# The second layer's input projection in seven half-depth products for eight, its operands, v, gates and decays waiting in DRAM

## The chip, the cores and the metric

The kernel runs on one core of a Trainium2 chip. A core has the engines TensorE (PE in the profile, with its weight loads as PEld), VectorE (DVE), ScalarE (ACT), GpSimd (POOL) and SyncE (SP), which here only issues DMAs. The metric is the time of one execution on the device in microseconds (us), less being better, given as the median of several runs. The profile is taken from one further execution.

## The reference: what is computed

An encoder of two layers works on 2048 tokens of width 1024. The first (even) layer mixes by a gated linear recurrence and short convolutions. The second (odd) one is a bidirectional gated linear attention with 4 heads; key width 128 and value width 256 per head. The part that matters:

```python
def odd_layer(x, norm_pre, norm_post, w_in, w_gate_lr, b_gate, head_norm_g, w_out):
    h = rmsnorm(x, norm_pre)
    proj = h @ w_in
    q, k, v, r, lr = jnp.split(
        proj, [GLA_KEY, 2 * GLA_KEY, 2 * GLA_KEY + GLA_VAL, 2 * GLA_KEY + 2 * GLA_VAL], axis=-1)
    ...
    z = jnp.einsum('bsdr,drk->dbsk', lr, w_gate_lr...) + b_gate[...]
    log_alpha = jax.nn.log_sigmoid(z) / GLA_NORMALIZER
    ...
    o_f = gla_chunked(qh, kh, vh, g_f)
    o_b = jnp.flip(gla_chunked(jnp.flip(qh, 2), ..., jnp.flip(g_b, 2)), 2)
    o = rmsnorm(o_f + o_b, head_norm_g)
    y = (o * jax.nn.silu(r.astype(jnp.float32))) @ w_out
    return (x + rmsnorm(y, norm_post)).astype(x.dtype)
```

`w_in` of this layer has 3104 columns: q and k (512 each), v and r (1024 each) and a rank part lr of 32, from which the decays `log_alpha` are made. x is 1024 wide on 2048 tokens.

## The kernel before

Activations lie transposed, with features on the 128 partitions and tokens along the free axis, in four chunks of 512 tokens. An fp32 operand of a projection is split into two f16 halves, hi and lo; a product is then three matmuls: weight hi by hi, weight hi by lo, weight lo by hi.

The stages, in order: the even layer's input projection, already made in seven half-depth products for eight (`mm3`, lines 794 to 796), with its operands waiting in DRAM; recurrences and convolutions beside it; the even output (`wo_mm`, lines 1123 to 1125), 1536 matmuls over chunks 0 to 3, each of eight groups (m) of 48 matmuls; beside it `post_even`, which norms each chunk, adds the residual and makes the operands H2 (hi, lo) of the second layer; the second layer's projections, `proj_atom` (lines 607, 608, 610) for q, k, r and the rank part, and `v_atom` (lines 1335 to 1337) for v; per head, `phase1` makes the decays from the rank part (a scan along the tokens, lines 1480 and 1483) and multiplies q and k by their exponentials, and `gla` makes scores (line 1557), transposes, states (1589) and outputs (1633, 1649, 1651); `gpost` and `gpost_out` norm a head's output, multiply by the gate and save it to DRAM; finally the output product (`wq_mm`, lines 1807 to 1809) with `post_odd` beside it.

The order of all instructions is made when the program is built. Each step of the work is a generator that says which engine it needs next ("P" TensorE, "A" ScalarE, "V" VectorE, "G" GpSimd, "D" a DMA) and for how long by a table of costs, and which events it waits for. The planner `Order` always takes the step that can start earliest, and among equals the one of better priority. Buffers come from pools: 22 large slots of 8 KB per partition with a cap for each role (H2 8, XR 2, V 3, E 4 and so on), eight PSUM banks, raw weight slots and pieces for split weights. The engines run their lists strictly in that order. All DMAs are on one queue, SP's, and are issued at line 279; line 250 is the helper of all ScalarE operations, 254 and 258 those of VectorE's.

The projections of the second layer serve as filler: the planner lays products of later heads between the attention matmuls of the present one. Weights are loaded and split (`WO`, `hl`, `WX` in the profile: high half by ScalarE, low half by VectorE) shortly ahead of their use. The gates r of head 3 are the last products in this order; `gate3` takes them. After the last head, `wq_split` splits the eight output weights.

Of the kernel before, what the change touches and what calls it, by code (L numbers as in the profile page):

```python
# [17 lines left out]
T = 2048  # L18
# [3 lines left out]
NSLOT = 22  # L22
# [135 lines left out]
def trunk_kernel(ctx: ExitStack, tc: tile.TileContext, xT, w_in, gate_w, w_out, odd_w, lr_w, lr_gw, odd_wo, params, outT):  # L158
# [18 lines left out]
        WO=8, YC=6, YB=2, XR=2, H2=8, LM=1, V=3, WX=2, QS=2, E=4, SB=1, O=2, G3=2, YL=1,  # L177
# [153 lines left out]
    def lam_consts():  # L331
# [25 lines left out]
        nc.vector.tensor_scalar(out=gsc[:, 16:24], in0=par[:, C_OPRE:C_OPRE + 8], scalar1=-2.0 ** -23, scalar2=None,  # L357
# [37 lines left out]
    pc_left = {i: 2 if i < 3 else 4 for i in range(5)}  # L395
# [16 lines left out]
    def pc_drop(i):  # L412
        pc_left[i] -= 1
        if pc_left[i] == 0:
            (wput if i < 3 else put)(PCT[i])
# [178 lines left out]

    def proj_atom(key, c, w, hh, cls="bg", ev2=None):
        b = yield from bank(cls)
        n = 0
        for hf in range(2):
            if hf and ev2 is not None:
                yield ("w", ev2)  # L600
            three = key[0] != "lr"
            yield ("P", (12 if three else 8) * 0.216)
            for kk in range(4):
                k = hf * 4 + kk
                hi, lo = hh[c][hf].t[:, kk, 0], hh[c][hf].t[:, kk, 1]
                wh, wl = w.s.t[:, 0, k], w.s.t[:, 1, k]
                nc.tensor.matmul(b.t, lhsT=wh, rhs=hi, start=(n == 0), stop=False)  # L607
                nc.tensor.matmul(b.t, lhsT=wh, rhs=lo, start=False, stop=(n == 7 and not three))  # L608
                if three:
                    nc.tensor.matmul(b.t, lhsT=wl, rhs=hi, start=False, stop=(n == 7))  # L610
                n += 1
        P[key, c] = b
        done(evP[key, c])
# [487 lines left out]
    def yc_loader():  # L1101
        yield ("w", evAlloc)
        for c in range(NCH):
            if c >= 2:
                yield ("w", evH2[c - 2])
            for q in range(4):
                s = yield from get("YC", [128, 4, 2, CH], F16)
                YC[c, q] = s
                for j in range(4):
                    ki = q * 4 + j  # L1110
                    yield ("w", evY[ki])
                    yield from dma(s.t[:, j], y_d[ki][:, :, c * CH:(c + 1) * CH], 256 * 1024)
                    done(evYC[c, ki])
# [53 lines left out]
    H2 = [[None, None] for _ in range(NCH)]  # L1167
    evH2 = [Ev() for _ in range(NCH)]
    XR = {}
    evXR = {(c, h): Ev() for c in range(NCH) for h in range(2)}  # L1170

    def xr_loader():
        yield ("w", evAlloc)
        yield ("w", ev_proj)
        for c in range(NCH):
            for hf in range(2):
# [17 lines left out]
    def post_even():  # L1194
        yield ("w", ev_proj)
        for c in range(NCH):
            yb = []
            for _ in range(2):
                s = yield from get("YB", [128, 4, CH])
                yb.append(s)  # L1200
# [19 lines left out]
            put(yb[1])  # L1220
            yield from rsq(r, b, 1.0 / (1024 * 4096), 1)
            put(yb[0])
            for hf in range(2):
# [3 lines left out]
                h = yield from get("H2", [128, 4, 2, CH], F16)  # L1227
                H2[c][hf] = h
                yield from act(h.t[:, :, 0], x, AF.Copy)
                yield from tt(h.t[:, :, 1], x, h.t[:, :, 0], ALU.subtract)  # L1230
                put(XR[c, hf])
# [12 lines left out]
    odd_order = [("lr", 0)]  # L1244
    for hd in range(4):
        if hd == 0:
            odd_order += [("q", hd), ("k", hd), ("va", hd), ("vb", hd)]
        if hd + 1 < 4:
            odd_order += [("q", hd + 1), ("k", hd + 1)]
        if hd < 2:  # L1250
            odd_order += [("va", hd + 1), ("vb", hd + 1), ("r", 2 * hd), ("r", 2 * hd + 1)]
        if hd == 2:
            odd_order += [("va", hd + 1), ("vb", hd + 1)]
    odd_order += [("r", i) for i in (4, 5, 6, 7)]
    for key in odd_order:
# [12 lines left out]
    items_odd = [(key, osrc(key)) for key in odd_order]  # L1268
    W["wz", 0] = Wt()
    items_odd.insert(3, (("wz", 0), lr_gw))  # L1270
    WV = {}
    evXput = [Ev() for _ in range(4)]
    evGLA = [Ev() for _ in range(4)]
    evWV = [Ev() for _ in range(4)]

    def w_split_odd():
        yield ("w", ev_proj)
        for key, _ in items_odd:
            w = W[key]
            if key[0] == "wz":  # L1280
                yield ("w", ev_wodone)
                s = yield from get("LM", [128, 2 * T], F16)
                mask = s.t[:, T:T + T // 2].bitcast(U8)
                LM[0] = (s.t[:, 0:T], mask)
                wz = s.t[:, T + T // 2:2 * T].rearrange("p (d n) -> p d n", d=2)
                WZ[0] = wz
                yield ("G", 2.0)
                nc.gpsimd.memset(mask, 1)
                nc.gpsimd.memset(mask.rearrange("p (n t) -> p n t", t=128)[:, :, 0:1], 0)
# [5 lines left out]
                done(w.ev)  # L1295
                continue
            if key[0] in ("va", "vb"):
                hd = key[1]
                if key[0] == "va":
                    yield ("w", ev_wodone)  # L1300
                    WV[hd] = yield from get("WX", [128, 8, 2, 256], F16)
                yield ("w", w.evr)
                o = 0 if key[0] == "va" else 128
                t = WV[hd].t
                yield from act(t[:, :, 0, o:o + 128], w.raw.t, AF.Copy, scale=1024.0)
                yield from stt(t[:, :, 1, o:o + 128], w.raw.t, 1024.0, t[:, :, 0, o:o + 128], ALU.mult, ALU.subtract)
                wput(w.raw)
                if o:
                    done(evWV[hd])
            else:  # L1310
                yield ("w", w.evr)
                w.s = yield from wget("hl", [128, 2, 8, 128], F16)
                yield from act(w.s.t[:, 0], w.raw.t, AF.Copy, scale=1024.0)
                if key[0] == "lr":

                    lo = w.s.t[:, 1, :, 96:128]
                    yield from stt(lo, w.raw.t[:, :, 96:128], 1024.0, w.s.t[:, 0, :, 96:128], ALU.mult, ALU.subtract)
                    yield from act(w.s.t[:, 0, :, 96:128], lo, AF.Copy)
                else:
                    yield from stt(w.s.t[:, 1], w.raw.t, 1024.0, w.s.t[:, 0], ALU.mult, ALU.subtract)  # L1320
                wput(w.raw)
                done(w.ev)

    def v_atom(hd, tp):

        b = yield from bank("bg", (128, 2, 256))
        for i in range(2):
            tk = tp * 2 + i
            c, o = tk // 4, (tk % 4) * 128
            yield ("P", 24 * 0.1095)  # L1330
            for k in range(8):
                h = H2[c][k // 4].t
                hi, lo = h[:, k % 4, 0, o:o + 128], h[:, k % 4, 1, o:o + 128]
                wh, wl = WV[hd].t[:, k, 0], WV[hd].t[:, k, 1]
                nc.tensor.matmul(b.t[:, i], lhsT=hi, rhs=wh, start=(k == 0), stop=False)  # L1335
                nc.tensor.matmul(b.t[:, i], lhsT=hi, rhs=wl, start=False, stop=False)  # L1336
                nc.tensor.matmul(b.t[:, i], lhsT=lo, rhs=wh, start=False, stop=(k == 7))  # L1337
        VP[hd, tp] = b
        done(evV[hd, tp])

    VP = {}
    evV = {(hd, tp): Ev() for hd in range(4) for tp in range(8)}
    ev_oproj = Ev()

    def bg_odd():
        yield ("w", ev_proj)

        def mt(key, cs):
            yield ("w", W[key].ev)
            for c in cs:  # L1350
                yield ("w", evH2[c])
                yield from proj_atom(key, c, W[key], H2)
            if cs[-1] == NCH - 1:
                wput(W[key].s)

        def vt(hd, tps):
            yield ("w", evWV[hd])
            for tp in tps:
                yield ("w", evH2[tp // 2])
                yield from v_atom(hd, tp)  # L1360

        for key in odd_order[:3]:
            yield from mt(key, [0, 1, 2])
        S.pools["ps"]["caps"].update(bg=4, fg=4)
        S.logs = True
        yield from vt(0, range(6))
        for key in odd_order[:3]:
            yield from mt(key, [3])
        yield from vt(0, range(6, 8))
        put(WV[0])  # L1370

        def rt(hd):
            ka, kb = ("r", 2 * hd), ("r", 2 * hd + 1)
            yield ("w", W[ka].ev)
            yield ("w", W[kb].ev)
            for c in CORD:
# [612 lines left out]
```

## Time and profile before

| | |
|---|---|
| median of 3 runs | 2254.71 us (2252.21 to 2256.13) |
| profiled execution | 2253.91 us |
| its span | 2252.2 us |
| mean granted TensorE clock | 0.994 |
| TensorE, VectorE, ScalarE busy | 97%, 61%, 54% |
| moved by DMA | 279.75 MB, mean 124 GB/s |
| even output begins, ends | about 1026, 1371 us |
| last outputs of the last head | about 2022 us |
| output product begins | 2070 us |

How to read it: "busy" is the sum of the durations of an engine's instructions. TensorE's matmuls are pipelined, so that the duration of one (0.38 us) is longer than the pitch from start to start (0.216 us); the pitch is what a matmul costs in a full stream. A row of a group names line, engine, operation, tile written and tiles read, shape, count, busy time, mean ns of one, and then the idle time just ahead with what ended it. A row of a DMA names the tiles, the count, the KB of each and the median us from issue to landing.

### The profile page before, as it was taken

To read this page: it belongs to the slowest core of one execution; us is meant where nothing else is said; L and a number is where in the kernel's file an instruction comes from. 1 tells how busy PE (TensorE), PEld (TensorE's weight loads), DVE (VectorE), ACT (ScalarE), POOL (GpSimd) and SP (SyncE) were. 2 spreads that over 40 slices of the span, in tenths; PEclk is the share of its full clock that TensorE was granted. 3 is DMA by queue.
4 is the path that set the end of the run, shared out by engine and by line. 5 is a ranking of instruction groups with operands and counts; after the bars stand their busy time and mean duration, and the time that the engine had idled before them with its cause. 6 is when DMAs were issued, how large, how long until landed. Compare 5 with 4: busy or idle time off the path is not lost.

```text
span 2252.2 us, 27779 instructions
## 1 busy us (share of the span) xinstructions
PE 2194.3 (97%) x11658; PEld 1185.3 (53%) x11658; DVE 1376.6 (61%) x1501; ACT 1206.9 (54%) x1566; POOL 2.8 (0%) x8
## 2 busy tenths in 40 slices
PE   5889999999999999999999999999999999999997
PEld 4334444444444444444444444768559558774446
DVE  7988788886776767674234344453733734656535
ACT  5567777866667666664122222546536636556322
POOL 0000000000000000000000000000000000000000
PEclk9999999999999999999999999999999999999999
DMA  7354453554535445369232221100020020005433
GB/s 263 141 222 173 166 203 124 192 187 150 218 136 200 178 165 219 131 238 315 73 131 75 78 73 66 47 10 11 24 71 1 17 68 10 15 15 183 156 109 113
DMA packets 87886, 279.75 MB, mean 124 GB/s; under 512 B 6737, under 2 KB 43729, under 8 KB 67537
## 3 DMA queue, kind: packets, MB, share of 16 engines
q1 hardware_dynamic: 87760, 277.98, 34.2%
q8 instruction: 91, 1.49, 0.3%
q14 instruction: 35, 0.28, 0.0%
HBM read 221.33 MB, written 56.62 MB: 123 GB/s over the span
## 4 chain that ended last, share of the span: by engine, by line
PE 85%; DVE 9%; ACT 3%; DMA 2%; issue 1%; SPq 0%; DVEq 0%; ACTq 0%
PE ps L796 11%; PE ps L794 11%; PE ps L795 11%; PE ps L1123 5%; PE ps L1124 5%; PE ps L1125 5%; PE ps L607 4%; PE ps L608 4%; PE ps L610 4%; PE ps L1808 2%; PE ps L1807 2%; PE ps L1809 2%; PE ps L1589 2%; DVE E L258 2%; PE ps L1335 2%; PE ps L1336 2%
## 5 line engine op out<-in xcount | busy, mean ns | idle before, releaser
L794 PE MATMUL ps<-H,PC 128*128 128x512 f16 (+1 forms) x744 | 280.5, 377 | 3.7 <-DMA H<-hd 2.9
L796 PE MATMUL ps<-H,PC 128*128 128x512 f16 (+1 forms) x744 | 280.4, 377 | 1.5 <-DVE PC L254 1.4
L795 PE MATMUL ps<-H,PC 128*128 128x512 f16 (+1 forms) x744 | 280.4, 377 | 0.0
L794 PE MATMUL ps<-H,hl 128*128 128x512 f16 (+1 forms) x648 | 244.4, 377 | 10.6 <-ACT H L250 7.3
L795 PE MATMUL ps<-H,hl 128*128 128x512 f16 (+1 forms) x648 | 244.3, 377 | 6.5 <-DVE H L258 6.5
L796 PE MATMUL ps<-H,hl 128*128 128x512 f16 (+1 forms) x648 | 244.6, 377 | 4.5 <-DVE hl L254 4.4
L607 PE MATMUL ps<-H,hl 128*128 128x512 f16 x544 | 206.8, 380 | 0.6 <-ACT QS L250 0.6
L608 PE MATMUL ps<-H,hl 128*128 128x512 f16 x544 | 206.7, 380 | 0.0
L610 PE MATMUL ps<-H,hl 128*128 128x512 f16 x512 | 194.4, 380 | 0.0
L1123 PE MATMUL ps<-YC,WO 128*128 128x512 f16 x512 | 194.1, 379 | 0.0
L1124 PE MATMUL ps<-YC,WO 128*128 128x512 f16 x512 | 194.0, 379 | 0.0
L1125 PE MATMUL ps<-YC,WO 128*128 128x512 f16 x512 | 194.0, 379 | 0.0
L1335 PE MATMUL ps<-WX,H 128*128 128x256 f16 x512 | 139.6, 273 | 0.0
L1336 PE MATMUL ps<-WX,H 128*128 128x256 f16 x512 | 139.6, 273 | 0.0
L1337 PE MATMUL ps<-WX,H 128*128 128x256 f16 x512 | 139.6, 273 | 0.0
L150 ACT ACT_TABLE_LOAD x95 | 121.9, 1283 | 1.6
L794 PEld LDWEIGHTS <-PC 128*128 128x128 f16 x744 | 72.8, 98 | 91.5 <-DMA H<-hd 4.7
L796 PEld LDWEIGHTS <-PC 128*128 128x128 f16 x744 | 72.8, 98 | 88.8 <-DVE PC L254 2.9
L795 PEld LDWEIGHTS <-PC 128*128 128x128 f16 x744 | 72.8, 98 | 85.9 <-issue 0.3
L796 PEld LDWEIGHTS <-hl 128*128 128x128 f16 x648 | 64.5, 100 | 85.8 <-issue 9.2
L1807 PE MATMUL ps<-YC,WO 128*128 128x512 f16 (+1 forms) x320 | 107.7, 337 | 0.0
L1808 PE MATMUL ps<-YC,WO 128*128 128x512 f16 (+1 forms) x320 | 107.7, 336 | 0.0
(227 smaller groups left out, 4052.5 us busy)
## 6 DMA issues: line engine op xcount, KB each, us to landing
H<-hd SPq DMA_DIRECT2D x112, 1024.0 KB, 5.9
raw<-w_in SPq DMA_DIRECT2D x48, 512.0 KB, 4.3
yd<-YH SPq DMA_DIRECT2D x16, 1024.0 KB, 4.9
YC<-yd SPq DMA_DIRECT2D x64, 256.0 KB, 4.8
hd<-H SPq DMA_DIRECT2D x14, 1024.0 KB, 4.9
raw<-odd_w SPq DMA_DIRECT2D x24, 512.0 KB, 3.7
raw<-w_out SPq DMA_DIRECT2D x16, 512.0 KB, 5.3
XR<-xT SPq DMA_DIRECT2D x8, 1024.0 KB, 8.1
```

The costliest lines, as they stand in the source:

```text
L607: nc.tensor.matmul(b.t, lhsT=wh, rhs=hi, start=(n == 0), stop=False)
L608: nc.tensor.matmul(b.t, lhsT=wh, rhs=lo, start=False, stop=(n == 7 and not three))
L610: nc.tensor.matmul(b.t, lhsT=wl, rhs=hi, start=False, stop=(n == 7))
L794: nc.tensor.matmul(b.t[:, sl], lhsT=wh, rhs=hi, start=s, stop=False, skip_group_check=True)
L795: nc.tensor.matmul(b.t[:, sl], lhsT=wh, rhs=lo, start=False, stop=False, skip_group_check=True)
L796: nc.tensor.matmul(b.t[:, sl], lhsT=wl, rhs=hi, start=False, stop=e, skip_group_check=True)
L1123: nc.tensor.matmul(b.t, lhsT=wh, rhs=hi, start=start, stop=False)
L1124: nc.tensor.matmul(b.t, lhsT=wh, rhs=lo, start=False, stop=False)
L1125: nc.tensor.matmul(b.t, lhsT=wl, rhs=hi, start=False, stop=stop)
L1335: nc.tensor.matmul(b.t[:, i], lhsT=hi, rhs=wh, start=(k == 0), stop=False)
L1336: nc.tensor.matmul(b.t[:, i], lhsT=hi, rhs=wl, start=False, stop=False)
L1807: nc.tensor.matmul(out, lhsT=wh, rhs=hi, start=start, stop=False)
```

## The change

The second layer's projections of q, k, r and v are made in seven products of half depth for eight, as the even layer's are. For a pair of output tiles and a pair of token chunks the eight products of four K-tiles become seven, on sums and differences of operands and of weights. It has these parts.

- **Operands.** `op2_make` and `op2_rest` make seven operands (hi, lo; 1 MB each) for chunks 0 and 1, and seven for 2 and 3, and save all 14 to DRAM. The first use of each half takes them where they were made; the later eight blocks reload them (`op2_loader`, 56 loads of 1 MB). XR's cap goes from 2 to 4, since sums need two chunks at once.
- **Weights.** `w_prep` makes, beside the even output, the sums of all 12 pairs of weight tiles (4 sums and 7 splits each) and saves the pieces (98 saves; those of v as two saves of 256-byte runs per piece and pair). `wu_loader` reloads them in order, and begins when all are prepared.
- **Products.** `seven` issues the seven products; its `copies` (ScalarE) and `sums` (VectorE) empty the banks, of which a unit takes four.
- **Order of the blocks.** `OBLK` says by hand which units of which half of the tokens follow each other. The gates are no longer the last products to be laid between attention matmuls: `r_out` applies SiLU at once and saves them (8 x 1 MB), and `g_loader` reloads them per chunk into YL.
- **Decays** are all made ahead (`decays`, both directions at once, all four heads), saved (8 x 1 MB) and reloaded in `phase1`. **v** of heads 1 to 3 is saved and reloaded too.
- Slots go from 22 to 23. The loads of the output weights wait for `evRaw`, the end of the weight preparation; `yc_loader` issues its loads as threads of their own.

The diff, cut:

```diff
-NSLOT = 22
+NSLOT = 23
...
-        WO=8, YC=6, YB=2, XR=2, H2=8, LM=1, V=3, WX=2, QS=2, E=4, SB=1, O=2, G3=2, YL=1,
+        WO=8, YC=6, YB=2, XR=4, H2=3, LM=1, WV=4, V=2, VD=2, XS=1, QS=2, E=4, SB=1, O=2, DQ=2, YL=2,
...
+    def op2_make(x, j, src):
+        s = yield from get("H2", [128, 4, 2, CH], F16)
+        yield from act(s.t[:, :, 0], src.t, AF.Copy)
+        yield from tt(s.t[:, :, 1], src.t, s.t[:, :, 0], ALU.subtract)
+        OP2[x, j] = s
+        done(evOp2[x, j])
+        S.spawn(op2_save(x, j), 3)
...
+    OBLK = [(0, [("qk", 0), ("v", 0)]), (1, [("v", 0), ("qk", 0), ("v", 1)]), (0, [("v", 1), ("r", 0)]),
+            (1, [("r", 0), ("qk", 1)]), (0, [("qk", 1), ("r", 1)]), (1, [("r", 1), ("qk", 2)]),
+            (0, [("qk", 2), ("r", 2)]), (1, [("r", 2), ("qk", 3)]), (0, [("qk", 3), ("r", 3)]), (1, [("r", 3)])]
...
+                def op(j, src, evo=evo, u=u, i=i, last=i == len(prs) - 1):
+                    p = yield from pget()
+                    yield from wsplit(p, src)
+                    S.spawn(w_save(u, j, i, p, last), 3)
+                    done(evo[j])
...
+                yield ("w", ra.evr)
+                yield ("w", rb.evr)
+                a11, a12 = ra.raw.t[:, 0:4], ra.raw.t[:, 4:8]
+                a21, a22 = rb.raw.t[:, 0:4], rb.raw.t[:, 4:8]
+                S.spawn(op(0, a11), 3)
+                S.spawn(op(2, a12), 3)
+                yield from tt(s, a21, a22, ALU.add)
+                S.spawn(op(1, s), 3)
+                S.spawn(op(5, a22), 3)
+                yield from tt(a21, a11, a21, ALU.subtract)
...
+    def wu_loader():
+        yield ("w", evPrep)
...
+            for n, b, s, a, i, op in (("C11", "B", "s1", 0, 0, ALU.add), ("C12", "E", "s2", 0, 1, ALU.add),
+                                      ("U3", "A", "s5", 1, 1, ALU.add), ("U3", "A", "s4", 1, 0, ALU.subtract)):
...
+        prod = (("A", True, "P1", None), ("E", True, "P5", None), ("B", True, "C11", None), ("A", False, "U2", "s1"),
+                ("E", False, "C12", "s5"), ("D", True, "P4", None), ("A", False, "U3", "s2"))
...
+    def r_out(h, x, s):
+        yield from act(s.t, s.t, AF.Silu)
+        yield from dma(r_d[h][x], s.t.rearrange("p a i t -> p a (i t)"), 2 ** 20)
...
+    def phase1(hd, d):
+        yield ("w", evGd[3, 0])
+        yield ("w", evGd[3, 1])
...
+        yield from dma(t2.t, g_d[hd, d], 2 ** 20)
+        yield from act(t1.t, t2.t, AF.Exp, scale=-1.0 / 16)
+        yield from act(t2.t, t2.t, AF.Exp, scale=1.0 / 16)
...
     def wq_loader():
+        yield ("w", evRaw)
```

Two places show what moves. On TensorE, at the end of the attention: in the kernel before, the last outputs of head 3 (lines 1649 and 1651) are followed by 216 projection matmuls (lines 607, 608, 610), and then comes the output product (1807).

```order
L1649 MATMUL ps_14377<-WX_13832,V_13621 128x128
L1651 MATMUL ps_14377<-E_13430,SB_13835 128x128
L607 LDWEIGHTS hl_12822
L607 MATMUL ps_14373<-H_817_9509,hl_12822 128x512
L608 LDWEIGHTS hl_12822
L608 MATMUL ps_14373<-H_817_9509,hl_12822 128x512
```

The same place now; 1889 and 1891 are the outputs, 2034 to 2036 the output product, WO its split weights and YC the gated head outputs loaded from DRAM.

```order
L1889 MATMUL ps_15053<-XS_14490,V_14309 128x128
L1891 MATMUL ps_15053<-E_14304,SB_14493 128x128
L2034 LDWEIGHTS WO_1403_15074
L2034 MATMUL ps_14995<-YC_1402_15073,WO_1403_15074 128x512
L2035 LDWEIGHTS WO_1403_15074
L2035 MATMUL ps_14995<-YC_1402_15073,WO_1403_15074 128x512
```

No projection matmul stands between outputs and output product any more. On VectorE at the same place, the kernel before: the last outputs are added (QS, first two rows), then gating (O), splits of the output weights (WO<-raw) and one of a gate weight (hl<-raw) alternate.

```order
L258 TENSOR_TENSOR QS_13833<-ps_14377,QS_13833 128x128
L258 TENSOR_TENSOR QS_13834<-ps_14377,QS_13834 128x128
L254 SCALAR_TENSOR_TENSOR O_12846<-O_12846,gsc,hv_13226 128x512
L258 TENSOR_TENSOR O_12846<-ps_14160,O_12846 128x512
L254 SCALAR_TENSOR_TENSOR WO_1295_14407<-raw_13230,WO_1295_14407 128x1024
L254 SCALAR_TENSOR_TENSOR YL_14026<-O_12846,YL_14026 128x512
L254 SCALAR_TENSOR_TENSOR hl_14426<-raw_12852,hl_14426 128x1024
L254 SCALAR_TENSOR_TENSOR WO_1295_14407<-raw_14413,WO_1295_14407 128x1024
```

And now, with the norm of head 3 (hv, ps) and its gating (QS, YL) between the splits:

```order
L258 TENSOR_TENSOR QS_14491<-ps_15053,QS_14491 128x128
L258 TENSOR_TENSOR QS_14492<-ps_15053,QS_14492 128x128
L258 TENSOR_TENSOR ps_14960<-ps_14960,hv_14952 128x512
L254 SCALAR_TENSOR_TENSOR hv_14952<-ps_14960,hv_14952 128x512
L254 SCALAR_TENSOR_TENSOR QS_14491<-QS_14491,gsc,hv_14952 128x512
L258 TENSOR_TENSOR QS_14491<-YL_14953,QS_14491 128x512
L254 SCALAR_TENSOR_TENSOR WO_1403_15074<-raw_14653,WO_1403_15074 128x1024
L258 TENSOR_TENSOR hv_14952<-ps_15080,hv_14952 128x512
L254 SCALAR_TENSOR_TENSOR YL_14953<-QS_14491,YL_14953 128x512
L254 SCALAR_TENSOR_TENSOR QS_14492<-QS_14492,gsc,hv_14952 128x512
L258 TENSOR_TENSOR hv_15087<-hv_14952,hv_15087 128x512
L258 TENSOR_TENSOR QS_14492<-YL_14953,QS_14492 128x512
```

From the addition of the last outputs to the eighth split VectorE's list now has 37 instructions of 512 columns and 8 splits of 1024; the first lies behind the first chunk's norm and gating.

More of the change, by code (lines that the diff above doesn't have):

```diff
@@ L393, in pieces @@
         done(ev_pc)
-    pc_left = {i: 2 if i < 3 else 4 for i in range(5)}
+    pc_left = {i: 2 if i in (0, 1, 2, 5, 6, 7, 8, 9) else 4 for i in range(10)}
     pc_closing = set()
@@ L593, in trunk_kernel @@
     evP = {}
[L595 to L613, printed above, removed]
     first = [("xa", 0), ("gc", 0), ("xb", 0), ("zb", 0)]
@@ L1324, in v_atom @@
[L1324 to L1339, printed above, removed]
@@ new lines, in trunk_kernel, with op2_loader @@
+    WVS = {}
+    BL2 = {}
+    evBl2 = {(b, j): Ev() for b in range(len(OBLK)) for j in range(7)}
+    def op2_loader():
+        for b, (x, _) in enumerate(OBLK):
+            for j in range(7):
+                if b < 2:
+                    yield ("w", evOp2[x, j])
+                    BL2[b, j] = OP2[x, j]
+                else:
+                    if b == 2 and j == 0:
+                        S.pools["slot"]["caps"].update(H2=7)
+                    yield ("w", evH2d[x][j])
+                    BL2[b, j] = yield from get("H2", [128, 4, 2, CH], F16)
+                    S.spawn(fetch(BL2[b, j].t, h2_d[x][j], 2 ** 20, evBl2[b, j]), 2)
+                    continue
+                done(evBl2[b, j])
@@ new lines, in fetch, with lr_mm @@
+    def fetch(out, in_, nbytes, ev):
+        yield from dma(out, in_, nbytes)
+        done(ev)
+    def lr_mm(c):
+        x = c // 2
+        b = yield from bank("bg")
+        terms = [(0, 0), (0, 1), (1, 4)] if c % 2 else [(0, 0), (1, 2)]
+        yield ("w", evLRP)
+        for i, (hf, j) in enumerate(terms):
+            yield ("w", evBl2[x, j])
+            yield ("P", 8 * 0.2157)
+            op, w = BL2[x, j].t, LRP[hf].t
+            for k in range(4):
+                for a in range(2):
+                    nc.tensor.matmul(b.t, lhsT=w[:, 0, k], rhs=op[:, k, a], start=(i == 0 and k == 0 and a == 0),
+                                     stop=(i == len(terms) - 1 and k == 3 and a == 1))
+        P[("lr", 0), c] = b
+        done(evP[("lr", 0), c])
@@ new lines, in v_save, with unit_v, alloc, after @@
+    def v_save(h, x):
+        yield from dma(v_d[h][x], V[h][x].t, 2 ** 20)
+        put(V[h][x])
+        done(evVs[h][x])
+    def unit_v(p, blk, wfin, ofin):
+        x = OBLK[blk][0]
+        hs = (2 * p, 2 * p + 1)
+        def alloc():
+            for h in hs:
+                if V[h][x] is None:
+                    V[h][x] = yield from get("V" if h == 0 else "VD", [128, 8, 256])
+        def after():
+            for h in hs:
+                if h == 0:
+                    count(("v", 0), 4, lambda: done(evVd[0]))
+                else:
+                    count(("v", h, x), 2, lambda: S.spawn(v_save(h, x), 3))
+        for s in range(2):
+            def dst(a, i, s=s):
+                return V[hs[a]][x].t[:, 4 * i + 2 * s:4 * i + 2 * s + 2]
+            yield from seven(("v", p), blk, s, alloc, dst, (U12, U12), after, wfin, ofin and s == 1)
+        if wfin:
+            for s in WVS["v", p]:
+                put(s)
+            if p:
+                done(evWVd)
```

605 lines of the change are left out of this document (366 added, 239 removed).

## The prediction

> **What bounds the kernel now.** The page comes first. TensorE is busy for 97% of the span, and the chain of waits lies on it for 85%.
>
> ```profile
> span 2252.2 us, 27779 instructions
> PE 2194.3 (97%) x11658; PEld 1185.3 (53%) x11658; DVE 1376.6 (61%) x1501; ACT 1206.9 (54%) x1566; POOL 2.8 (0%) x8
> PE 85%; DVE 9%; ACT 3%; DMA 2%; issue 1%; SPq 0%; DVEq 0%; ACTq 0%
> ```
>
> The profiled execution took 2253.91 us, 1.7 more than its span and 0.8 less than the median of the runs, 2254.71. My sums are made against 2253.91. About 0.2%, 4.5 us, is what a measurement here tells from no change.
>
> An average over the span says nothing of one stage, so I cut it where the PE lines change: even output (from 1026), start of the second layer (1371), attention heads (1490), products left over after the last head (2023), output product (2070). The columns are the window, its length, then busy time and instructions of PE, weight load, VectorE (DVE), ScalarE (ACT) and GpSimd; then the granted clock, the DMA engines' share and GB/s.
>
> ```profile
> 1026.00:1371.00 345.00, 345.00 (x1598) 156.81 (x1597) 126.01 (x125) 92.33 (x114) 1.97 (x2) 1.00 0.32 107
> 1371.00:1490.00 119.00, 118.39 (x741) 72.65 (x740) 68.30 (x49) 55.19 (x67) 0.00 (x0) 1.00 0.17 57
> 1490.00:2023.00 533.00, 530.37 (x3555) 386.90 (x3554) 267.96 (x380) 283.52 (x477) 0.00 (x0) 1.00 0.08 24
> 2023.00:2070.00 47.00, 47.00 (x219) 21.49 (x218) 27.38 (x35) 27.99 (x40) 0.00 (x0) 1.00 0.52 161
> ```
>
> From 1026 to 2070 TensorE idles 0.61 + 2.63 = 3.2 us of 1044. Every matmul taken out there is worth its whole pitch, as long as nothing else comes late. VectorE has 37% in the even output, 57%, 50% and 58% after it; the DMA queue has most of its time free. This slack is what the change spends.
>
> **The gain: matmuls taken out.** Seven products of half depth stand for eight. From the instruction orders, the second layer's input projection had 1600 matmuls of 512 columns and 1536 of 256; now it has 1424 and 1344 (the rank projection grows from 64 to 80 within the first number). The pitch, start to start, is read from two stretches of the timeline:
>
> ```profile
> 1200.79 0.38 PE L607 MATMUL ps<-H,hl 128*128 128x512 f16 x1
> ...
> 1204.03 0.38 PE L608 MATMUL ps<-H,hl 128*128 128x512 f16 x1
> 1402.82 0.27 PE L1335 MATMUL ps<-WX,H 128*128 128x256 f16 x1
> ...
> 1404.89 0.27 PE L1336 MATMUL ps<-WX,H 128*128 128x256 f16 x1
> ```
>
> Fifteen steps in 3.24 us are 0.216 each; nineteen in 2.07 are 0.109. So 176 x 0.216 + 192 x 0.109 = 38.0 + 20.9 = **58.9 us** less. The new 512-column products have the old shape, so I give them the old pitch.
>
> **What is added on the other engines.** VectorE and ScalarE durations, then the DMAs:
>
> ```profile
> L258 DVE TENSOR_TENSOR E<-E,QS 128x2048 f32<-128x2048 f32 x16 | 36.1, 2281 | 9.4 <-ACT E L250 9.4
> L1480 DVE TENSOR_TENSOR_SCAN E<-LM,E 128x2048 f32<-128x2048 uint8 x4 | 17.7, 4425 | 0.2
> L254 DVE SCALAR_TENSOR_TENSOR XR<-XR,gsc,hv 128x512 f32<-128x512 f32 x32 | 21.9, 746 | 0.1
> L254 DVE SCALAR_TENSOR_TENSOR hl<-raw,hl 128x512 f16<-128x512 f32 x56 | 38.0, 685 | 11.1 <-ACT hl L250 11.0
> L254 DVE SCALAR_TENSOR_TENSOR WO<-raw,WO 128x1024 f16<-128x1024 f32 x8 | 9.8, 1224 | 6.7 <-ACT WO L250 6.6
> L250 ACT ACTIVATE hl<-raw 128x512 f16<-128x512 f32 x56 | 34.4, 622 | 10.9 <-PE ps L795 7.8 <-DVE raw L258 2.7 <-DMA raw<-w_in 0.3
> L250 ACT ACTIVATE E<-E 128x2048 f32<-128x2048 f32 x32 | 61.1, 1910 | 0.4
> ```
>
> ```profile
> H<-hd SPq DMA_DIRECT2D x112, 1024.0 KB, 5.9
> yod<-YL SPq DMA_DIRECT2D x32, 256.0 KB, 2.5
> YC<-yod SPq DMA_DIRECT2D x32, 256.0 KB, 4.7
> raw<-odd_w SPq DMA_DIRECT2D x24, 512.0 KB, 3.7
> 1000.00:1050.00 50.00, 47.79 (x222) 21.31 (x221) 29.11 (x33) 24.15 (x24) 0.00 (x0) 1.00 0.96 352
> ```
>
> *Beside the even output* go twelve weight pairs. Each has 4 sums and 7 low halves on VectorE, 11 x 0.685 = 7.5 us, or 90 in all; 7 high halves on ScalarE, 7 x 0.622 = 4.4; two loads of 3.7 and seven saves of 2.5 on the queue. VectorE there rises from 126 to about 225 of 345 us, since the operand work moves in too. A pair has 345 / 12 = 28.7 us. So the stage holds on average, and I charge nothing for it but its end. There the second ones product of chunk 2 has slipped from ahead of group 3 to inside group 5 of chunk 3. Until chunk 3's first bank is emptied, VectorE does eight scalings of 0.746 and four of 0.685, and ScalarE two steps of about 0.62 between them: 10 us, against 36 matmuls, 7.8 us, left to run. With semaphores I take **4 us**, between nothing and 6. All twelve pairs should be ready about 4 us ahead of the end, and the first reloaded weights are wanted some 9 us behind it, after the rank product (40 x 0.216 = 8.6). That is the cover, and a rival below prices its loss.
>
> *Operands of the second half.* The seven of chunks 2 and 3 are made of eight-fold sums of 2.28 us each on VectorE while TensorE already uses the first. By the chain of their making the second is ready about when it is wanted: **2 us** (0 to 5).
>
> *Decays.* All eight are made in the first 115 us of the second layer, instead of two per head. On VectorE each takes 2.28 + 4.43 + 2.28 = 9.0 us, so 72 us of that stretch, beside the emptying of banks, which TensorE waits for. ScalarE has two passes of 1.9 for each, 30 us in the same stretch. A wait of a bank behind one scan is at most 4.4 us and the product before it covers 2.6; four such make **6 us** (3 to 12).
>
> *Head changes.* Between the last outputs of a head and the next scores TensorE has 171, 219 and 134 products: 36.9, 47.3 and 28.9 us. Within the last, the shortest, VectorE has four multiplications (9.1) and twenty instructions of 0.685 (13.7); ahead of the multiplications stand a load of 1 MB (5.9) and two exponentials (3.8) that before needed no load, since they were computed in place. 22.8 + 9.7 = 32.5, with some overlap: 26 to 36 against 28.9. I take **9 us** for the three, between 0 and 30.
>
> *Reloads.* 56 loads of 1 MB bring each block its operands: at 352 GB/s 3.0 us each, seven per block of about 57 us or more. They fit; where v and decay loads stand ahead in the in-order queue, the first is late: **2 us** (0 to 8). The 14 saves of operands, the 6 and 6 MB of v and the 8 and 8 MB of gates and decays lie in the same free time of the queue (0.08 to 0.17 busy).
>
> *The tail.* Before, 216 projection matmuls, 216 x 0.216 = 46.7 us, stood between the last head's outputs and the output product:
>
> ```profile
> 2070.09 0.38 PE L1807 MATMUL ps<-YC,WO 128*128 128x512 f16 x1
> ```
>
> Under them ran the last head's normalization, the split of the eight output weights and the first loads. Now nothing stands there; the gates were taken earlier. The last outputs are followed at once by the first block, eight steps of 12 matmuls, 20.7 us. But before the eighth step VectorE has, in its order, 8 splits of 1.224 and 37 instructions of 0.685: 9.8 + 25.3 = 35.1 us. The eighth step then takes 2.6 more, so the block ends 37.7 us after the outputs at best; with three ones products TensorE has about 23.4 us of its own. The queue is no better: saves of 2.5 and loads of 4.7 alternate there. **15 us** (12 to 20).
>
> These make 4 + 2 + 6 + 9 + 2 + 15 = 38 us.
>
> **The clock after a wait.** Long waits cost more than themselves, as early rows show (the bracket is the idle time ahead):
>
> ```profile
> 81.97 0.58 PE L795 MATMUL ps<-H,hl 128*128 128x512 f16 x1 [2.54 <-DVE H L258]
> 82.34 0.63 PE L796 MATMUL ps<-H,hl 128*128 128x512 f16 x1
> ...
> 85.76 0.63 PE L795 MATMUL ps<-H,hl 128*128 128x512 f16 x1
> 86.94 0.38 PE L796 MATMUL ps<-H,hl 128*128 128x512 f16 x1
> 82.00:84.00 2.00, 2.00 (x5) 0.66 (x5) 2.00 (x1) 1.08 (x2) 0.00 (x0) 0.50 0.00 0
> ```
>
> After 2.54 us of idling the granted clock is 0.50 and the pitch (85.76 - 82.34) / 8 = 0.428; some eleven matmuls lose 0.21 each, 2.3 us. I expect three waits of that length (end of the even output, last head change, first steps of the tail): 3 x 2.3 = **7 us**, between 0 and 14.
> [...]
>
> **Sum.** -58.9 + 38 + 7 = -14 against 2253.91: **2240 us**. With the bounds of the single waits added as independent errors, the case's own range is 2222 to 2257.
>
> **Rivals.**
>
> *All covers hold.* Every small wait vanishes in slack, and only the tail, at its low end, 12 us minus what early weights save, remains: 2253.91 - 58.9 + 8 = 2203. For it speaks that TensorE's longest waits between 1371 and 2070 are so far these (total, count, longest):
>
> ```profile
> PE ps L456 <- ACT hv L250: 2.2, 1, 2.2
> PE ps L607 <- ACT QS L250: 0.6, 1, 0.6
> ```
>
> Against it speaks that VectorE's sum in the tail, 35.1 us, is in the order and can't be hidden by nothing. Chance 0.15.
>
> *VectorE becomes the bound of the heads.* In the second layer it has 68 + 268 + 27 = 363 busy us of 699. To these come 96 sums of 0.685 (66) and about 20 of operand work, and 22 splits of 1.224 (27) go: about 422 of 640, 52% to 66%. Should each of its in-order rows at the head changes and decays wait for a load or ScalarE, the heads cost not 9 but 21 and the decays 12 of my range: +18, so 2258. The decider is the cover of 28.9 to 47.3 us. Chance 0.13.
>
> *Slower: the weights come late.* All reloads wait for the end of the whole preparation. The chain of one pair is load, sum, high half, low half, save, with two raw slots and few pieces, and the queue is shared with the even output's own loads. Should each of twelve pairs need 5 us over its 28.7, the end moves by 60, and after the slack of 4 + 9 us TensorE stands for 47: 2240 + 47 = 2287. It decides from a preparation that ends 9 us behind the last even-output matmul; a net loss needs about 23. For it: seven saves of 2.5 are 17.5 us of a pair's 28.7, and no slot is free until they land. Against it: loads, VectorE and saves overlap, and the DMA share is only 0.32 there. Chance 0.18.
> [...]
>
> *The change does less than it says:* the matmuls are counted in the order, so I give this nothing of its own.
>
> **How the numbers follow.** Forecast 0.54, covers hold 0.15, VectorE bound 0.13, weights late 0.18. Faster by over 0.2% means below about 2250: 0.50 + 0.15 + 0.03 = 0.68. Within: 0.03 + 0.05 + 0.02 = 0.10. Slower: 0.01 + 0.05 + 0.16 = 0.22. The range goes from 2203, the middle of the best case, to 2268, above VectorE's case; left out are most of the late weights and half of the best case, 0.2.
>
> **What would show it right or wrong.** Right: TensorE busy about 59 us less; idle of TensorE in the second layer of 35 to 45 us, of which 12 to 20 stand behind the last head's outputs with VectorE split rows as releaser; a few windows with a clock of 0.5 to 0.9. Wrong: a gap of over 10 us at the end of the even output, released by a weight load; head changes idle for over 10 us each; a tail without a gap; or 256-byte saves far over 2.5 us.

## The result and the profile after

The changed kernel takes 2228.2 us (median of 4 runs, 2225.38 to 2228.67) against 2253.46 of the kernel before: ratio 0.9884, 95% interval 0.9867 to 0.9901. The forecast was 2240 within 2203 to 2268, and faster. Measured once more, beside the later experiments, the same kernel gave 0.9907 (0.9890 to 0.9925). The two differ by 0.2%, so the experiments are read by their profiles as much as by their ratios; each ratio is to the kernel before as it was measured beside that run.

The page of the changed kernel; its span is 25.8 us shorter.

```profile
span 2226.4 us, 27957 instructions
PE 2142.4 (96%) x11290; PEld 1151.8 (52%) x11290; DVE 1518.4 (68%) x1720; ACT 1254.4 (56%) x1636; POOL 2.8 (0%) x8
PE 78%; DVE 10%; DMA 6%; ACT 3%; issue 2%; SPq 1%; DVEq 0%; ACTq 0%
```

TensorE is busy 2194.35 - 2142.37 = 52.0 us less, and idles 26 us more. It has 11658 - 11290 = 368 matmuls fewer, the 176 + 192 that were forecast. The DMA, 2% of the chain before, now has 6% of it. The same cuts by stage: even layer, even output, start of the second layer (two windows), heads, tail, output product.

```profile
0.00:200.00 200.00, 160.35 (x791) 80.33 (x792) 165.49 (x202) 120.07 (x129) 0.79 (x6) 0.96 0.55 207
200.00:1022.00 822.00, 817.81 (x3787) 369.95 (x3786) 636.29 (x614) 578.16 (x637) 0.00 (x0) 1.00 0.49 185
1022.00:1366.00 344.00, 338.74 (x1556) 153.19 (x1555) 217.90 (x260) 140.42 (x196) 1.98 (x2) 1.00 0.64 214
1366.00:1485.00 119.00, 117.42 (x876) 85.69 (x875) 80.33 (x66) 53.91 (x70) 0.00 (x0) 1.00 0.44 173
1485.00:1628.00 143.00, 138.42 (x968) 95.00 (x966) 82.14 (x57) 77.72 (x98) 0.00 (x0) 0.99 0.75 288
1628.00:2026.00 398.00, 392.35 (x2346) 269.68 (x2344) 231.67 (x400) 215.96 (x384) 0.00 (x0) 1.00 0.58 213
2026.00:2065.00 39.00, 28.11 (x98) 11.71 (x99) 35.48 (x51) 21.23 (x32) 0.00 (x0) 0.82 0.73 232
2065.00:2226.00 161.00, 149.18 (x880) 86.25 (x877) 69.06 (x75) 46.91 (x94) 0.00 (x0) 0.97 0.38 133
```

For the comparison, the windows of the kernel before that were not shown yet:

```profile
0.00:200.00 200.00, 161.50 (x772) 79.85 (x773) 170.98 (x202) 118.72 (x128) 0.79 (x6) 0.96 0.54 201
200.00:1026.00 826.00, 822.03 (x3806) 371.79 (x3805) 628.72 (x612) 571.55 (x633) 0.00 (x0) 1.00 0.49 183
2070.00:2252.00 182.00, 170.06 (x976) 95.84 (x973) 87.24 (x102) 57.60 (x110) 0.00 (x0) 0.98 0.39 133
```

Length less busy is TensorE's idle time in a window. After minus before, with the prediction's terms beside:

| stage | idle after | idle before | more | predicted |
|---|---|---|---|---|
| even layer, to 1022 (1026) | 43.8 | 42.5 | 1.3 | 0 |
| even output | 5.3 | 0.0 | 5.3 | 4 |
| operands, decays, to 1628 | 6.2 | 0.6 | 5.6 | 2 + 6 |
| heads and reloads | 5.7 | 2.6 | 3.0 | 9 + 2 |
| tail and output product | 22.7 | 11.9 | 10.8 | 15 |
| sum | | | 26.0 | 38 |

Less busy time: 58.9 of matmuls taken out, by their pitch, less a rest of 58.9 - 52.0 = 6.9, which I put down to matmuls at a slow clock (predicted 7). So -52.0 + 26.0 = -26.0, within 0.2 of the difference of the spans.

The three largest waits in the changed kernel's second layer (total, count, longest):

```profile
PE ps L2034 <- DMA YC<-yod: 10.5, 3, 6.3
PE ps L774 <- DMA H<-gd: 4.1, 1, 4.1
PE ps L774 <- ACT QS L250: 3.0, 1, 3.0
```

The largest is in the tail, and it ends with a load of head outputs (YC), not with a split of output weights. The tail on TensorE's timeline, first from its last outputs (L1891) on:

```profile
2024.24 0.39 PE L1891 MATMUL ps<-E,SB 128*128 128x128 f32 x2
2030.95 0.58 PE L2034 MATMUL ps<-YC,WO 128*128 128x512 f16 x1 [6.32 <-DMA YC<-yod]
...
2042.81 0.38 PE L2034 MATMUL ps<-YC,WO 128*128 128x512 f16 x1 [3.38 <-DMA YC<-yod]
```

And the one DMA queue (SPq) in the same stretch: the start of each issue. The gates r of head 3 are saved as rd and reloaded into YL.

```profile
2020.35 0.33 SPq L279 DMA_DIRECT2D rd<-DQ  x1
...
2025.15 0.57 SPq L279 DMA_DIRECT2D YL<-rd  x1
2025.77 0.60 SPq L279 DMA_DIRECT2D YC<-yod  x1
2030.82 0.34 SPq L279 DMA_DIRECT2D raw<-odd_wo  x1
2032.02 0.56 SPq L279 DMA_DIRECT2D yod<-YL  x1
2032.62 0.61 SPq L279 DMA_DIRECT2D YC<-yod  x1
...
2036.89 0.65 SPq L279 DMA_DIRECT2D YC<-yod  x1
```

What the queue itself waited for between 2018 and 2070 us (total, count, longest):

```profile
SPq L279 <- DVE WO L254: 13.2, 5, 4.4
SPq L279 <- DVE YL L254: 12.8, 8, 3.2
SPq L279 <- DMA rd<-DQ: 3.9, 1, 3.9
```

The first YC load is issued 1.5 us after the last outputs, and TensorE gets it 5 us later. It shows no wait of its own: it follows at once on the reload of a gate (YL<-rd), which waited 3.9 us until the save of the gates (rd<-DQ) had landed. The next ones carry results of heads that were saved long ago. They are still issued 4 to 7 us apart, since each stands behind a raw load, which waits for a buffer that VectorE's split frees, and most also behind a save (yod) that waits for VectorE's gating.

### The profile page after: what moved, and what is told of

Read it like the earlier page. It is cut to its first block, busy times and chain, and to the rows that moved or that the text cites. A ratio compares the mean times of both kernels' runs of the same rounds, so it can differ in the third digit from the quotient of the medians.

```text
span 2226.4 us, 27957 instructions
## 1 busy us (share of the span) xinstructions
PE 2142.4 (96%) x11290; PEld 1151.8 (52%) x11290; DVE 1518.4 (68%) x1720; ACT 1254.4 (56%) x1636; POOL 2.8 (0%) x8
## 4 chain that ended last, share of the span: by engine, by line
PE 78%; DVE 10%; DMA 6%; ACT 3%; issue 2%; SPq 1%; DVEq 0%; ACTq 0%
PE ps L774 15%; PE ps L776 15%; PE ps L775 15%; PE ps L1103 3%; PE ps L1104 3%; PE ps L1105 3%; PE ps L2034 2%; PE ps L2036 2%; PE ps L2035 2%; PE ps L1829 2%; PE ps L1492 2%; PE ps L1494 2%; PE ps L1493 2%; DVE H L258 2%; DMA raw<-odd_w 1%
## 5 line engine op out<-in xcount | busy, mean ns | idle before, releaser
L774 PE MATMUL ps<-H,hl 128*128 128x512 f16 (+1 forms) x896 | 337.5, 377 | 14.2 <-ACT H L250 5.2
L775 PE MATMUL ps<-H,hl 128*128 128x512 f16 (+1 forms) x896 | 337.4, 377 | 4.3 <-DVE H L258 4.3
L776 PE MATMUL ps<-H,hl 128*128 128x512 f16 (+1 forms) x896 | 337.3, 376 | 3.9 <-DVE hl L254 3.7
L774 PE MATMUL ps<-H,PC 128*128 128x512 f16 (+1 forms) x752 | 283.4, 377 | 4.2 <-DMA H<-hd 3.2
L776 PE MATMUL ps<-H,PC 128*128 128x512 f16 (+1 forms) x752 | 283.3, 377 | 0.6 <-DVE PC L254 0.6
L775 PE MATMUL ps<-H,PC 128*128 128x512 f16 (+1 forms) x752 | 283.3, 377 | 0.0
L775 PEld LDWEIGHTS <-hl 128*128 128x128 f16 x896 | 88.4, 99 | 113.2 <-issue 15.0
L776 PEld LDWEIGHTS <-hl 128*128 128x128 f16 x896 | 88.4, 99 | 112.0 <-issue 7.0
L774 PEld LDWEIGHTS <-hl 128*128 128x128 f16 x896 | 88.5, 99 | 103.3 <-issue 3.9
L1492 PE MATMUL ps<-WV,H 128*128 128x256 f16 x448 | 122.1, 273 | 1.8 <-ACT VD L250 1.8
L1493 PE MATMUL ps<-WV,H 128*128 128x256 f16 x448 | 122.1, 273 | 0.0
L1494 PE MATMUL ps<-WV,H 128*128 128x256 f16 x448 | 122.1, 273 | 0.0
L2034 PE MATMUL ps<-YC,WO 128*128 128x512 f16 (+1 forms) x320 | 110.0, 344 | 10.5 <-DMA YC<-yod 10.5
L2036 PE MATMUL ps<-YC,WO 128*128 128x512 f16 (+1 forms) x320 | 110.2, 344 | 0.0
L2035 PE MATMUL ps<-YC,WO 128*128 128x512 f16 (+1 forms) x320 | 109.8, 343 | 0.0
```

What stands on the lines that cost most here:

```text
L774: nc.tensor.matmul(b.t[:, sl], lhsT=wh, rhs=hi, start=s, stop=False, skip_group_check=True)
L775: nc.tensor.matmul(b.t[:, sl], lhsT=wh, rhs=lo, start=False, stop=False, skip_group_check=True)
L776: nc.tensor.matmul(b.t[:, sl], lhsT=wl, rhs=hi, start=False, stop=e, skip_group_check=True)
L1492: nc.tensor.matmul(b.t[:, i], lhsT=hi, rhs=wh, start=st, stop=False, skip_group_check=True)
L2034: nc.tensor.matmul(out, lhsT=wh, rhs=hi, start=start, stop=False)
L2035: nc.tensor.matmul(out, lhsT=wh, rhs=lo, start=False, stop=False)
```

## The experiments

Three theories of the tail were open. *VectorE's list*, as predicted: 35 us of work must be done before the eighth step. *The queue*: long-ready loads stand behind rows that wait. *Cover*: whatever the chain is, it hurts only because no filler stands there. Beside the tail, the rivals of the prediction were tried.

**Without low halves: VectorE's list shortened.**

```diff
-            yield from stt(t[:, 1], WQR[k].t, 1024.0, t[:, 0], ALU.mult, ALU.subtract)
...
-        wh, wl = wt[:, 0, m * 128:(m + 1) * 128], wt[:, 1, m * 128:(m + 1) * 128]
+        wh = wl = wt[:, 0, m * 128:(m + 1) * 128]
```

> Leaves out the low halves of the output weights (the high half is used in their place), so 8 x 1.22 = 9.8 us of VectorE work go from the tail; loads and ScalarE's halves stay. VectorE's list as the bound: the first block of the output product ends 8 to 10 us earlier, the time falls by 8 to 10 us. The queue's loads as the bound (a wait for a load ended the first step and the third): at most 3 us.

Measured: ratio 0.9920 (0.9903 to 0.9936), so no gain. From the last outputs to the last matmul of the output product it takes 2216.9 - 2027.6 = 189.3 us, against 2213.0 - 2024.4 = 188.6 in the changed kernel. VectorE now has time to spare in the same window (28.86 busy of 39 instead of 35.48; this run's tail starts 3 us later in it):

```profile
2026.00:2065.00 39.00, 25.05 (x98) 11.24 (x97) 28.86 (x45) 24.53 (x37) 0.00 (x0) 0.82 0.78 257
```

Its longest wait of TensorE in the tail:

```profile
PE ps L2033 <- DMA YC<-yod: 12.2, 3, 6.4
```

The wait for YC is as long as before, 12.2 us instead of 10.5. So the 9.8 us of VectorE's splits don't set the tail by themselves, as the prediction had it. VectorE's list isn't far from it either: in the changed kernel its eighth split starts at 2062.24, takes 1.22 us and ends about when the eighth step begins (2063.33), but the step shows no wait for it.

**Throwaway matmuls in the first wait.**

```diff
     def bg_wq():
         yield ("w", ev_oproj)
+        yield ("w", evGLA[3])
+        b = yield from bank("fg", (128, 4, 128))
+        yield ("P", 0.1)
+        for i in range(54):
+            nc.tensor.matmul(b.t[:, i % 4], lhsT=ident, rhs=ident, start=True, stop=True)
+        unbank(b)
```

> 54 throwaway matmuls (128x128, about 6 us) stand between the last outputs and the first output product; nothing else changes. If the clock's fall after the 6.3 us wait is a price of its own, the first block ends 3 us earlier and the time falls by 3 us. If VectorE's list (45 instructions, ending with the eighth split) sets the end of the block, the matmuls of the first steps run at 0.216 instead of 0.43, the next waits grow by as much, and the time stays within 1 us.

Measured: 0.9927 (0.9912 to 0.9942), 0.2 to 0.4% worse than the changed kernel. The experiment missed its size: 54 fp32 products are 108 rows and took 12.0 us, twice what I planned. Measured from the last outputs, the first step began 2038.0 - 2025.8 = 12.2 us behind them instead of 2030.9 - 2024.4 = 6.5, so 5.7 us late.

```profile
L2044 PE MATMUL ps<-ident x108: 275/275/276, 2025.9 to 2037.9; 128*128 128x128 f32 x108
```

The wait for YC that is left:

```profile
PE ps L2034 <- DMA YC<-yod: 2.2, 2, 1.2
```

The output product ends 4.5 us later (2218.9 - 2025.8 = 193.1 against 188.6), so only 1.2 of the 5.7 are swallowed. A separate price of the clock isn't settled by this run. Nor does it decide about VectorE's list: its eighth split, too, starts later behind the last outputs, 2066.78 - 2025.8 = 41.0 us for 2062.24 - 2024.4 = 37.8.

**Early splits and loads.**

```diff
     def wq_split():
-        yield ("w", evGLA[3])
+        yield ("w", evLast)
...
     def yc2_loader():
-        yield ("w", evGLA[3])
+        yield ("w", ev_oproj)
```

evLast is set when the last block's operands have been asked for.

> The splits of the output weights may start as soon as the last block's operands have been asked for, and the loads of the head outputs when the last projection product is issued, instead of after the last head. By the instruction order four of eight splits then stand ahead of the last outputs. VectorE's list as the bound: 4 x 1.22 = 5 us of the tail go, and the first loads land earlier, so the first wait of 6.3 us shrinks to under 2; together 7 to 10 us faster. If head 3 needs those slots or VectorE's time itself, nothing is gained, 0 to 3.

Measured: 0.9864 (0.9849 to 0.9880), 2221.3 us. Its span is 2218.6, 7.8 below that of the changed kernel. The first wait is gone; two are left:

```profile
2034.91 0.38 PE L2036 MATMUL ps<-YC,WO 128*128 128x512 f16 x1 [2.05 <-DMA YC<-yod]
2041.54 0.59 PE L2036 MATMUL ps<-YC,WO 128*128 128x512 f16 x1 [3.87 <-DMA YC<-yod]
```

By the ratios it is 0.2 to 0.4% faster than the changed kernel, 4.5 to 10 us for the 7 to 10 expected. Splits and loads were moved together, so this run doesn't say which of them gave it. The first row also shows a wait of 2.05 us without slow matmuls behind it, the second one of 3.87 with them.

**The last head's saves on another queue.**

```diff
-        yield from dma(yo_d[i][:, :, sl], y, 256 * 1024)
+        yield from dma(yo_d[i][:, :, sl], y, 256 * 1024, nc.gpsimd if i >= 6 else None)
```

> Only the 8 saves of the last head's gated outputs go on GpSimd's DMA queue instead of SyncE's; order and work of all engines stay. Queue theory: in the tail the loads of head outputs that have long been in DRAM stand on the one queue behind saves that wait for VectorE (12.8 us of waiting there), so without them the waits after the first (3.4 and 0.8 us, with slow clock behind) go, and 3 to 7 us are gained; the first wait of 6.3 us stays, since it begins when the slots come free. Rival, VectorE's list as the bound: within 1 us.

Measured: 0.9909 (0.9891 to 0.9926), with the unaltered kernel beside it at 0.9907. From last outputs to last matmul 2212.0 - 2024.2 = 187.8 us against 2213.8 - 2024.1 = 189.7 there.

```profile
2034.90 0.34 SPq L279 DMA_DIRECT2D raw<-odd_wo  x1
2035.33 0.52 SPq L279 DMA_DIRECT2D YL<-rd  x1
2035.90 0.61 SPq L279 DMA_DIRECT2D YC<-yod  x1
```

The queue theory's 3 to 7 us did not come. The expectation lets the first wait begin when slots come free; the trace shows the load behind the reload of a gate there, as in the changed kernel. With the saves gone, the loads still stand behind raw loads that wait for their buffers. The run without low halves freed those buffers early and left the saves. Each takes one holder of the queue away and leaves the other; neither gains. The next run takes both away.

**Both: early loads, and the saves on GpSimd's queue.**

The edit is that of the two runs together.

> Early splits and loads of the tail together with the saves of the last head on GpSimd's queue. With early loads alone two waits for loads are left (2.0 and 3.9 us). Queue theory: both go, 4 to 8 us below early loads alone, about 2213 to 2217. Rival: the rows of the last head itself come late (their norm and gating on VectorE), the waits stay: within 2 us of early loads alone.

Measured: 0.9868 (0.9850 to 0.9885), 2219.86 us, the same as early loads alone. Waits of 1.3 and 3.5 us for YC stay, in front of the third and the fourth step (2033.18 and 2039.47). The loads of these two steps on the queue:

```profile
2027.30 0.33 SPq L279 DMA_DIRECT2D rd<-DQ  x1
2027.67 0.52 SPq L279 DMA_DIRECT2D YC<-yod  x1
...
2032.23 0.52 SPq L279 DMA_DIRECT2D YL<-rd  x1
2032.80 0.76 SPq L279 DMA_DIRECT2D YC<-yod  x1
```

The size is the rival's, its reason is not: the third and fourth step use rows of head 1, long since saved. All raw loads are issued before the last outputs here and the last head's saves are on the other queue, but a third holder is left: the save of head 3's gates, for which the queue waits 9.3 us until ScalarE has made them, and their reload, which waits 2.5 us for that save. So the in-order queue is the best account of the tail, with three kinds of rows that hold it. No run takes all three away, so it isn't proven. Either of the two is the fastest version found, 1.3% below the kernel before.

**Cover put back.**

```diff
         for blk, (x, us) in enumerate(OBLK):
+            if blk == len(OBLK) - 1:
+                yield ("w", evGLA[3])
```

> The last block (the second half of the gates of head 3, 84 to 168 matmuls, 18 to 36 us) is held back until the last head's outputs are issued, so that it stands again between outputs and output product. Cover theory: the waits of the tail (10.9 us and about 7 us of slow clock) mostly vanish and head 3 loses little: 8 to 15 us faster. Rival: the products were needed as filler beside head 3's attention and its waits come to light there: within 5 us or slower.

Measured: 0.9886 (0.9871 to 0.9900), the time of the changed kernel. The waits for YC are gone; what is left in front of the output product's steps is small, and ends with splits of output weights. The window of the heads, then the waits:

```profile
1628.00:2026.00 398.00, 389.19 (x2318) 268.08 (x2317) 239.53 (x412) 217.28 (x390) 0.00 (x0) 0.99 0.57 209
```

Waits in the tail:

```profile
PE ps L2038 <- DVE WO L254: 2.6, 3, 1.7
PE ps L2036 <- ACT WO L250: 2.3, 2, 1.7
```

In the window of the heads, idle time went from 5.65 to 8.81 us. A wait of 2.2 us for ScalarE (E) is new there, and the waits for a reload (H<-gd) are 5.2 us instead of 4.1. Cover cures the tail's YC waits, but the filler is missed in the heads. Both theories of this run were half right; the span is 2.3 us shorter (2224.1), less than can be told.

**The unaltered kernel again**, the measure for the runs beside it (queue, both, whole lines):

> The changed kernel unaltered, as the measure for the runs of the same call: ratio to the kernel before 0.987 to 0.990, tail waits as before (6.3 us and 3.4 us for loads of head outputs).

Measured: 2229.26 us, ratio 0.9907. The waits for YC are 12.1 us in all, the longest 6.5 and 2.2.

**Decays in place.**

```diff
-        S.spawn(decays(0), 3)
-        S.spawn(decays(1), 3)
...
+        yield from act(t1.t, t2.t, AF.Exp, scale=-1.0 / 16)
+        yield from act(t2.t, t2.t, AF.Exp, scale=1.0 / 16)
```

`phase1` makes its decays itself, as in the kernel before; nothing of them is saved.

> The changed kernel with the decays made per head again, in place, without saving and reloading them (16 MB less on the queue). If making all eight ahead costs waits at the start of the second layer (5.5 us were seen from 1366 to 1628), 3 to 6 us faster. Rival: the scans, 4 x 4.4 us a head, come back to the head changes, whose cover is now 28.9 to 47.3 us, and TensorE waits there: 10 to 40 us slower.

Measured: 1.0087 (1.0072 to 1.0102), 2269.93 us, slower than the kernel before.

```profile
PE ps L1782 <- DVE E L258: 24.0, 2, 21.6
```

TensorE waits 21.6 us at one head change for a product behind the scans. The rival is right: with fewer products between heads, decays must lie ahead. That they cost the 5.6 us at the start of the second layer isn't shown: without them TensorE idles there (1366 to 1480 us) 114.00 - 105.65 = 8.4 us.

**Saves of the weights doubled.**

```diff
+        yield from dma(d2[:, :, :, i * 128:i * 128 + 128] if u[0] == "v" else d2, p.t, 256 * 1024)
+        yield from dma(d, p.t, 256 * 1024)
         pput(p)
```

> Every prepared piece of weights is saved twice (98 more saves of 256 KB, the second holds the piece until it landed). It doubles the suspected cost of the slower rival. If the preparation has slack, under 5 us slower and no gap at the end of the even output. If the preparation is close to its deadline, each pair takes up to 5 us more and a gap of 20 to 47 us released by a weight load opens there.

Measured: 1.0051 (1.0036 to 1.0066), 2262.49 us, 34 above the changed kernel's 2228.2. The traces count 84 saves of pieces (28 each for q and k, for v and for r), not 98, and as many again here. The gap is where the slower rival put it:

```profile
1405.83 0.58 PE L774 MATMUL ps<-H,hl 128*128 128x512 f16 x1 [26.44 <-DMA hl<-wdqk]
```

In the changed kernel the first reload is issued, on the queue's timeline, at

```profile
1365.17 1.29 SPq L279 DMA_DIRECT2D raw<-wdqk  x3
```

takes 3.5 us to land, the median of its kind, and the first product begins, on TensorE's timeline, at

```profile
1373.84 0.38 PE L774 MATMUL ps<-H,raw 128*128 128x512 f16 x1
```

Slack: 1373.84 - 1365.17 - 3.5 = 5 us of the 4 + 9 that I gave it. The rival's mechanism is real; 84 more saves were enough to make the kernel slower than before.

**Less preparation.**

```diff
+    LAST = {("r", 2): ("r", 1), ("r", 3): ("r", 1)}
...
         for u in UNITS:
+            if u in LAST:
+                continue
...
```

> Leaves out the preparation of the last two units (gates of heads 2 and 3 use the weights of head 1): 22 VectorE instructions, 15 us, and 14 saves less beside the even output; all products stay. If VectorE's crowding there made the 5.3 us of waits for the ones products, they fall to about 2.2, the value of before: 3 us faster. If not, within 1 us.

Measured: 0.9933 (0.9917 to 0.9950). The ones products wait 3.4 us for VectorE and 3.0 for ScalarE instead of 3.1 and 2.2. So the last weight pairs are not what these waits come from. The changed kernel's own windows say why the run was aimed at the wrong place: the idle time lies at the norms of earlier chunks, and the last 66 us of the stage, where those pairs are made, have none.

```profile
1100.00:1200.00 100.00, 96.82 (x438) 43.29 (x435) 59.23 (x73) 39.02 (x55) 0.00 (x0) 0.98 0.70 207
1200.00:1300.00 100.00, 97.92 (x452) 44.50 (x453) 75.00 (x81) 42.12 (x58) 0.00 (x0) 1.00 0.60 212
1300.00:1366.00 66.00, 66.00 (x307) 29.99 (x306) 48.76 (x60) 27.70 (x41) 1.98 (x2) 1.00 0.57 205
```

What makes the ones products late at those norms stays open. The planner also laid the tail otherwise (2219.2 - 2026.6 = 192.6 us of it), which accounts for 4 us of the loss.

**Whole lines for v.**

```diff
-        yield from dma(d[:, :, :, i * 128:i * 128 + 128] if u[0] == "v" else d, p.t, 256 * 1024)
+        yield from dma(d[i] if u[0] == "v" else d, p.t, 256 * 1024)
...
```

> The saves of v's prepared pieces write whole lines of 2 KB per partition instead of runs of 256 bytes; their reloads then write runs of 256 bytes in the on-chip memory. If the short runs made the saves slow (3.5 us median, against 2.6 for q, k and 2.1 for the gates), they fall to 2.1 to 2.6. The time stays within 2 us, since no weight load was waited for; if preparation sits at its deadline, up to 5 us faster.

The first row is the changed kernel's, the second this one's:

```profile
wdv<-hl SPq DMA_DIRECT2D x28, 256.0 KB, 3.5
```

```profile
wdv<-hl SPq DMA_DIRECT2D x28, 256.0 KB, 2.1
```

The runs of 256 bytes cost a factor 3.5 / 2.1 = 1.7 against lines of 2 KB. The time, 0.9892 (0.9870 to 0.9913), can't be told from 0.9907: the saves weren't on the path.

**The slot alone.** The kernel before with `NSLOT = 23`.

> The kernel before with 23 slots for 22, nothing else. The even layer reached its output 3.6 us earlier in the changed kernel, with the same matmuls. If the 23rd slot (and the other order that the planner then finds) gives this, the time is 2 to 5 us below the kernel before and the even output begins at 1022; if it comes from something else in the change, the time stays within 1 us.

Measured: 0.9995 (0.9985 to 1.0004). The profile shows the even output beginning at 1021.9, as in the changed kernel, but of the 3.9 us only 1.1 is seen in the medians of ten and thirteen runs. The edit has a second part that the expectation doesn't name: it sets `dynamic_dma_scratch_size=4096`, as the changed kernel does. So the earlier start belongs to one of these two or to the order that follows from them, and not to the seven products; its worth is under what can be told.

## Why the prediction was right, point by point

- *The gain of 58.9 us* fits: 368 matmuls fewer and 52.0 less busy are measured. The rest of 6.9 is a difference; by the count below, slow clock explains about 5 of it.
- *The clock's 7 us* came out in size by luck. Counted on the timelines, from matmuls of 512 columns that the next follows after up to 0.43 us for 0.216, the changed kernel loses about 10 us behind the even layer: 5.5 in three falls in the tail, and 1.5 to 1.7 in each of three others (at 1149, 1624 and 1733 us). The kernel before loses 1.2 there. Against that, in the first 200 us, with those of 256 columns counted too, the kernel before loses 8.5 and the changed one 4.5. I had three falls of 2.3 and nothing for the even layer.
- *The even output's end, 4 us:* the stage's 5.3 us come near only by chance. They lie at 1100 to 1300, at the ones products of earlier norms; at the end, where I saw VectorE's work hold up a bank, there is none. That step failed: the bank's wait was covered.
- *Operands and decays, 8 us:* measured 5.6, but hardly by the mechanism. I had banks waiting behind VectorE's scans. The waits name ScalarE for 3.0 us (QS) and 1.8 (VD) and VectorE for 1.4 (H); the 3.0 stand behind four exponentials of the first head, 7.6 us, and a SiLU of 1.9 on ScalarE. That decays must lie ahead holds: in place, the span is 42 us longer (2268.8 - 2226.4).
- *Head changes and reloads, 11 us:* measured 3.0. This term was mis-sized most. I added up VectorE's list, a load and exponentials as if they hardly overlapped, 32.5 us against a cover of 28.9; no score waits longer than 0.2 us. The one large wait in that stretch is 4.1 us for a reload (H<-gd), which I had at 2. There the rival that all covers hold was nearer.
- *The tail, 15 us:* measured 10.8 of idling, about 16 with its slow clock; the size is luck. The step "before the eighth step VectorE has 35.1 us" failed as the cause: 9.8 us less of it changed nothing, and the waits end with loads of head outputs, not with VectorE's splits as my sign of being right had it. In its place stands, as far as is shown, the in-order queue, with the gates' save and reload ahead of the first load, and raw loads and saves ahead of the next.
- *The rival of late weights* got 0.18. TensorE had 5 us of slack; in the run with doubled saves it used that up and 26.4 us more. That chance wasn't too high.

The forecast gain was 14 us and the measured one 25. The forecast's 12 us of excess are 8 in the heads, 4 in the tail and 2 in the decays, less 3 in the even layer and the even output.

## What to carry to other kernels

When matmuls leave a kernel that hides everything under them, ask where the last filler stood. An engine's work list gives a lower limit; another chain can be as long, and then shortening the list gains nothing. On one in-order queue, look first for a ready load that stands behind a row that waits for something else, and after each repair look again for the next such row. A preparation that must be done by a date needs its slack read in the trace: here it was 5 us, and a preparation some 30 us later turned 25 us gained into a loss.

## What the runs showed of the hardware that was not expected

- In these runs no one length of a wait tells whether the clock falls behind it. Behind single waits of 3.38, 3.54, 3.87 and 6.32 us in the tails matmuls followed each other after 0.43 us for 0.216, and not behind 2.05 and 2.21 (early loads; the unaltered kernel again). But in the changed kernel a single wait of 2.95 us gave a fall, and in the queue run the same wait gave none, the next matmul following at its old pitch (1624.20) and the granted clock from 1366 to 1628 us being 1.00 there, for 0.99 in the changed kernel. First row the changed kernel, second the queue run:

```profile
1623.68 0.59 PE L774 MATMUL ps<-H,hl 128*128 128x512 f16 x1 [2.95 <-ACT QS L250]
1623.98 0.38 PE L774 MATMUL ps<-H,hl 128*128 128x512 f16 x1 [2.95 <-ACT QS L250]
```

The prediction's row of 2.54 us had another wait of 2.06 at 79.05, just ahead of it, with one matmul between, which I had overlooked; so that row doesn't show what 2.54 us alone does. What decides stays open.
- The fall can come late. In the combined version four matmuls after the wait kept their pitch of 0.21 us, and then came the slow ones:

```profile
2039.47 0.38 PE L2036 MATMUL ps<-YC,WO 128*128 128x512 f16 x1 [3.54 <-DMA YC<-yod]
...
2040.33 0.58 PE L2037 MATMUL ps<-YC,WO 128*128 128x512 f16 x1
```
